# Decay factors of a gated DeltaNet: from triangle products on TensorE to running sums, a broadcast by way of DRAM, and an exponential with a bias per token

## The chip, the cores and the metric

The kernel runs on one core of a Trainium2 chip. The metric is the time of one execution in device microseconds (us), as the median of several runs. The profile shows one execution of the same program; its engines are called PE (TensorE, with PEld for its weight loads), DVE (VectorE), ACT (ScalarE), POOL (GpSimd) and SP (SyncE, which issues most of the DMAs).

## The reference

One decoder layer on 256 tokens of 2048 channels in float32: RMSNorm, one input projection, two token mixers side by side, gates, an output projection, and then a gated MLP of width 5632. What the change touches lies in the first mixer, a gated delta rule with 16 heads of 128 channels. Per head and token there is a log decay g (never positive) and a rate beta:

```
g_log = -exp(a_log) * softplus(a_raw + dt_bias)          # (256 tokens, 16 heads)
g     = cumsum(g_log within a chunk)
decay[i, j] = exp(g[i] - g[j])   for j <= i, else 0
lmat  = strictly lower part of (beta_i k_i . k_j) * decay
attn  = (q_i . k_j) * decay
```

`lmat` goes into a triangular solve, `attn` into the output. The reference walks chunks of 64 tokens with a state between them. The decay between any two tokens, however they are chunked, is the exponential of the sum of `g_log` over the tokens after j up to i.

## The kernel before, in words

The 256 tokens are two tiles of 128 (t = 0, 1). There is no state: the kernel builds the whole 256 by 256 lower triangle of each head from two tiles, `dec0` (source token j in tile 0 on the partitions, target token i in 0 to 255 along the row) and `dec1` (source and target both in tile 1). `dec0` therefore has a triangular block (targets 0 to 127) and a full block (targets 128 to 255).

The work is a sequence of large products. `gemm_a` (L138) multiplies the 256 tokens by 512 columns of a weight matrix. Each weight piece of 256 x 512 is loaded by SP into one of four `raw` buffers (L110), cast by ACT into `whi` (L112) and its rest is taken by DVE into `wlo` (L119), with three buffers for each of the two; PE then runs twelve products of 512 columns on the piece (L149 to L151). Pieces are prepared two ahead of PE.

The mixing part runs over four groups g of four heads: K, Q, V, the pooling input, its gate, a small pooling product, Z and the other gate. The delta rule of a group is a generator, `gdn` (L445). It is stepped by `side()` twice per weight piece, so that its small products, evictions and DVE work are written between the large products. The order on each engine is not exactly the written one: a planner with its own model of the times puts an instruction where it thinks its inputs are ready, the earlier written one first, and each engine then executes its own list strictly in that order, as does SP with its DMAs.

The places that matter here:

- L294 to L304: masks made by POOL and DVE at the start. `tri` is 1 where the column is at or after the partition, `low` is 1 where the column is before it, `onesr` and `lowr` are float32r copies.
- L381: `glog`, the log decays, tokens on partitions, 2 tiles by 16 heads; it comes at the end of a chain of some 25 small DVE instructions.
- L384 to L393: `glog` split in a float32r part `ghi` and the rest `glo`, and one small product with `low` (L391) for `tail`, the sum over the tokens of tile 0 after the source token.
- L455 to L484: the decays of a group, two heads at a time. DVE multiplies `tri` by the log decay of each source token (L464, L465, four instructions for each of the two parts), PE multiplies these by `lowr` or `onesr` (L472, L473, L475: the triangle products, six for two heads), ACT takes exponentials out of PSUM (L476, L477, L480), POOL zeroes the upper triangles (L482).
- L491 and L493: products of keys with keys and queries; L506 and L510: DVE multiplies these by `dec0`, `dec1` and a factor per token.
- L520 to L568: a block inverse of the triangular matrix. It sends small tiles through DRAM (`cdd`, `lb`, `tbd`, `tct`) on SP's queue. `tct` and `tcm` share buffers with two of the products of L465.
- L654 and L716: the output `on` of a group uses the buffer of `dec0`; L716 is its last reader. `psg` is a pool of four PSUM banks that all the small products share.

Of the kernel before, what the change touches and what calls it, by code (L numbers as in the profile page):

```python
# [26 lines left out]
B0 = 32  # L27
# [6 lines left out]
def kernel(  # L34
# [20 lines left out]
    nc = tc.nc  # L55
    mm = nc.tensor.matmul
# [4 lines left out]
    dpool = ctx.enter_context(tc.tile_pool(name="dram", bufs=2, space=bass.MemoryType.DRAM))  # L61
# [118 lines left out]
    ones = cpool.tile([P, P], F32, name="ones")  # L180
# [3 lines left out]
                            channel_multiplier=1)  # L184
# [7 lines left out]
    mp = mix.__enter__()  # L192
# [17 lines left out]
    for k2 in range(KD // 2):  # L210
# [6 lines left out]
        for kk in range(2):  # L217
# [3 lines left out]
                                           op0=ALU.mult, op1=ALU.subtract)  # L221
# [59 lines left out]
    for c in range(4):  # L281
        for t in range(2):
# [8 lines left out]
    nc.vector.tensor_scalar(rsq, rs1, 0.25, None, op0=ALU.mult)  # L291


    tri = mp.tile([P, P], F32, name="tri")  # L294
    nc.gpsimd.affine_select(tri, ones, pattern=[[1, P]], compare_op=ALU.is_ge, fill=0.0, base=0,
                            channel_multiplier=-1)
    low = mp.tile([P, P], F32, name="low")
    nc.gpsimd.affine_select(low, ones, pattern=[[-1, P]], compare_op=ALU.is_gt, fill=0.0, base=0,
                            channel_multiplier=1)

    onesr = mp.tile([P, P], F32R, name="onesr")
    nc.vector.tensor_copy(onesr, ones)
    lowr = mp.tile([P, P], F32R, name="lowr")
    nc.vector.tensor_copy(lowr, low)  # L304

    def same_block(b, name, tag):
        e = mp.tile([P, P // b, b], F32, tag=tag, name=name)
# [10 lines left out]
    for cq in range(4):  # L318
        pr = slice(32 * cq, 32 * cq + 32)
        nc.gpsimd.affine_select(idb[pr], ones[pr, 0:1].unsqueeze(2).to_broadcast([32, 8, B0]),  # L320
                                pattern=[[-1, 8], [1, B0]], compare_op=ALU.is_equal, fill=0.0, base=-8 * cq,
                                channel_multiplier=0)
# [57 lines left out]
    glog = mp.tile([P, 2, NH], F32, name="glog")  # L380
    nc.vector.tensor_tensor(glog, lp, ea.unsqueeze(1).to_broadcast([P, 2, NH]), op=ALU.mult)  # L381


    ghi = mp.tile([P, 2, NH], F32R, name="ghi")  # L384
    nc.vector.tensor_copy(ghi, glog)
    glo = mp.tile([P, 2, NH], F32, name="glo")
    nc.vector.tensor_tensor(glo, glog, ghi.bitcast(F32), op=ALU.subtract)


    psd = pg([P, NH])  # L390
    mm(psd, low, glog[:, 0, :], start=True, stop=True)  # L391
    tail = mp.tile([P, NH], F32, name="tail")
    nc.vector.tensor_copy(tail, psd)  # L393

    bands = mp.tile([P, 4, NB], F32, name="bands")
    for g, win in enumerate(WINDOWS):
# [3 lines left out]
        for cs in (slice(0, P + PAD), slice(P + PAD, NB)):  # L403
            b = bd[:, cs]
            n = cs.stop - cs.start
# [39 lines left out]
    def gdn(g, kq, vT, res):  # L445
# [6 lines left out]
        sj = mp.tile([P, 2, 4], F32, tag="sj", name=nm("sj"))  # L452
        dec0 = mp.tile([P, 4, S], F32, tag="dec0", name=nm("dec0"))
        dec1 = mp.tile([P, 4, P], F32, tag="dec1", name=nm("dec1"))
        for hp in range(2):  # L455

            h0 = 2 * hp
            rx = []
            for part, gp in (("h", ghi.bitcast(F32)), ("l", glo)):
                r0 = mp.tile([P, 2, P], F32R, tag="r0" + part, name=nm("r0"))  # L460
                r1 = mp.tile([P, 2, P], F32R, tag="r1" + part, name=nm("r1"))
                for i in range(2):
                    hh = 4 * g + h0 + i
                    nc.vector.tensor_scalar(r0[:, i], tri, gp[:, 0, hh : hh + 1], None, op0=ALU.mult)  # L464
                    nc.vector.tensor_scalar(r1[:, i], tri, gp[:, 1, hh : hh + 1], None, op0=ALU.mult)  # L465
                rx.append((r0, r1))
            yield
            pd0 = pg([P, 2, P])
            pdx = pg([P, 2, P])
            pd1 = pg([P, 2, P])  # L470
            for n, (r0, r1) in enumerate(rx):
                mm(pd0, lowr, r0, start=(n == 0), stop=(n == 1))  # L472
                mm(pd1, lowr, r1, start=(n == 0), stop=(n == 1))  # L473
            for n, (r0, r1) in enumerate(rx):
                mm(pdx, onesr, r1, start=(n == 0), stop=(n == 1))  # L475
            nc.scalar.activation(dec0[:, h0 : h0 + 2, 0:P], pd0, AF.Exp)  # L476
            nc.scalar.activation(dec1[:, h0 : h0 + 2, :], pd1, AF.Exp)  # L477
            for i in range(2):
                hh = 4 * g + h0 + i
                nc.scalar.activation(dec0[:, h0 + i, P:S], pdx[:, i, :], AF.Exp, bias=tail[:, hh : hh + 1])  # L480
            for d in (dec0[:, h0 : h0 + 2, 0:P], dec1[:, h0 : h0 + 2, :]):
                nc.gpsimd.affine_select(d, d, pattern=[[0, 2], [1, P]], compare_op=ALU.is_ge, fill=0.0, base=0,  # L482
                                        channel_multiplier=-1)
            yield  # L484
        for hp in range(2):
            h0 = 2 * hp
            hs = slice(h0, h0 + 2)
# [55 lines left out]
        tbd = dpool.tile([32, 4, 8 * B0], F32, tag="tbd", name=nm("tbd"))  # L543
        for cq in range(4):
            nc.sync.dma_start(tbd[:, cq], tb[32 * cq : 32 * cq + 32].rearrange("p c i -> p (c i)"))
        tct = mp.tile([P, 8, B0], F32, tag="r1l", name=nm("tct"))
        nc.sync.dma_start(tct, tbd.rearrange("(q r) a (c i) -> q (r a c) i", q=8, i=B0).rearrange("q p i -> p q i"))

        for h in range(4):
# [5 lines left out]
                nc.scalar.activation(vt[:, t, h, :], pvt[:, t, :], AF.Copy, scale=nk[:, t, h : h + 1])  # L555
        for _ in range(WAIT - 3):
            yield
        tcm = mp.tile([P, 8, B0], F32, tag="r1h", name=nm("tcm"))
        nc.vector.transpose(tcm.rearrange("p q c -> p (q c)"), tct.rearrange("p q c -> p (q c)"))
        Ta = mp.tile([P, 8, P], F32, tag="T", name=nm("T"))  # L560
        TTa = mp.tile([P, 8, P], F32, tag="TT", name=nm("TT"))
# [342 lines left out]
```

## Time and profile before

| what | value |
|---|---|
| time, median of 3 runs | 1582.16 us (1582.14 to 1584.18) |
| the profiled execution: its own time, its span | 1581.35 us, 1579.6 us |
| mean granted TensorE clock | 0.997 |
| DVE, ACT, POOL busy | 1040.2 us (66%), 745.8 us (47%), 89.4 us (6%) |
| DMA | 314.61 MB, mean 199 GB/s |

Busy time counts an engine as occupied from the start to the modelled end of each instruction. Products on PE overlap, so that the step from one start to the next is shorter than the duration of one. A row of the groups gives line, engine, operation, tiles, shapes and count, then the total busy time, the mean of one in ns, and the idle time in front of it with the one that ended it. A row of a timeline gives start, duration up to the end of the last merged instruction, and what it is. A row of the waits gives who waited for whom, the total, the number of times and the longest.

### The profile page before, as it was taken

The page shows a single profiled execution, that of the slowest core. Times are in us where ns is not written, and L with a number is a line of the kernel's source. Part 1 is how long each engine was busy: PE and PEld are TensorE (multiplying, and loading weights), DVE is VectorE, ACT ScalarE, POOL GpSimd, SP SyncE. Part 2 cuts the span into 40 slices and gives each one's busy share as a digit, 9 for nine tenths or more (in the row PEclk, how much of TensorE's full clock was granted, in tenths as well). Part 3 has the DMA queues.
Part 4 walks back from the last instruction along what each step waited for, and adds up shares of the span by engine and source line. Part 5 has one row for each costly group of instructions (what it writes and reads, how often), then busy time and mean ns, then how long its engine had stood idle before and what let it go on. Part 6 is the DMA issues. An engine that isn't in the chain of part 4 may idle for free.

```text
span 1579.6 us, 20017 instructions
## 1 busy us (share of the span) xinstructions
PE 1556.7 (99%) x7408; PEld 1284.3 (81%) x7408; DVE 1040.2 (66%) x1544; ACT 745.8 (47%) x925; POOL 89.4 (6%) x121
## 2 busy tenths in 40 slices
PE   8999999999999999999999999999999999999997
PEld 6878888888888888787888888888788878888885
DVE  5778757786678757795655666665666666444445
ACT  6545436444545435454454455444454445434344
POOL 3020100100010100102000000000000000000000
PEclk9999999999999999999999999999999999999998
DMA  7656656665556655565555878788777787755553
GB/s 253 181 155 195 193 148 173 167 197 173 155 153 190 197 149 175 164 191 176 198 188 187 238 224 243 242 244 247 232 234 251 230 246 234 239 196 191 196 191 132
DMA packets 263736, 314.61 MB, mean 199 GB/s; under 512 B 109894, under 2 KB 124246, under 8 KB 263510
## 3 DMA queue, kind: packets, MB, share of 16 engines
q1 hardware_dynamic: 260928, 308.85, 64.5%
q10 hardware_dynamic: 2710, 4.48, 0.8%
q8 instruction: 58, 0.95, 0.2%
q14 instruction: 40, 0.33, 0.1%
HBM read 298.61 MB, written 14.68 MB: 198 GB/s over the span
## 4 chain that ended last, share of the span: by engine, by line
PE 86%; DMA 4%; DVE 4%; issue 3%; SPq 1%; POOL 1%; ACT 0%; DVEq 0%; POOLq 0%
PE psm L151 22%; PE psm L150 21%; PE psm L149 21%; PE psg L840 3%; PE psm L839 3%; PE psg L839 2%; PE psm L838 2%; PE psg L838 2%; PE psm L840 2%; DVE wlo L119 2%; DMA gs<-flip 1%; SPq L162 1%; PE psg L491 1%; DMA flip<-tn 1%; PE psg L175 1%
## 5 line engine op out<-in xcount | busy, mean ns | idle before, releaser
L119 DVE TENSOR_TENSOR wlo<-raw,whi 128x1024 fp32r<-128x1024 f32 x528 | 648.5, 1233 | 376.1 <-ACT whi L112 368.6
L112 ACT CAST whi<-raw 128x1024 fp32r<-128x1024 f32 x530 | 556.9, 1053 | 716.2 <-PE psm L150 548.2
L151 PE MATMUL psm<-wlo,xhl 128*128 128x512 f32 x896 | 353.1, 394 | 2.1 <-DVE wlo L119 2.1
L149 PE MATMUL psm<-whi,xhl 128*128 128x512 f32 x896 | 352.3, 393 | 1.3 <-ACT xhl L219 1.3
L150 PE MATMUL psm<-whi,xhl 128*128 128x512 f32 x896 | 351.9, 393 | 0.0
L151 PE MATMUL psm<-wlo,fhl 128*128 128x512 f32 x704 | 273.7, 390 | 1.9 <-DVE wlo L119 1.4
L150 PE MATMUL psm<-whi,fhl 128*128 128x512 f32 x704 | 274.0, 389 | 0.0
L149 PE MATMUL psm<-whi,fhl 128*128 128x512 f32 x704 | 273.9, 389 | 0.0
L151 PEld LDWEIGHTS psm<-wlo,xhl 128*128 128x128 f32 x896 | 168.6, 188 | 37.8 <-DVE wlo L119 3.7
L149 PEld LDWEIGHTS psm<-whi,xhl 128*128 128x128 f32 x896 | 168.7, 188 | 35.4 <-ACT xhl L219 1.7
L150 PEld LDWEIGHTS psm<-whi,xhl 128*128 128x128 f32 x896 | 168.7, 188 | 34.7
L151 PEld LDWEIGHTS psm<-wlo,fhl 128*128 128x128 f32 x704 | 132.1, 188 | 32.0 <-DVE wlo L119 4.8
L150 PEld LDWEIGHTS psm<-whi,fhl 128*128 128x128 f32 x704 | 132.2, 188 | 27.6
L149 PEld LDWEIGHTS psm<-whi,fhl 128*128 128x128 f32 x704 | 132.2, 188 | 27.1
L838 PE MATMUL psg<-whi,hhi 128*128 128x512 f32 x176 | 68.5, 389 | 0.0
L838 PE MATMUL psm<-whi,hhi 128*128 128x512 f32 x176 | 68.5, 389 | 0.0
L839 PE MATMUL psm<-whi,hlo 128*128 128x512 f32 x176 | 68.5, 389 | 0.0
L839 PE MATMUL psg<-whi,hlo 128*128 128x512 f32 x176 | 68.5, 389 | 0.0
L840 PE MATMUL psm<-wlo,hhi 128*128 128x512 f32 x176 | 68.5, 389 | 0.0
L840 PE MATMUL psg<-wlo,hhi 128*128 128x512 f32 x176 | 61.1, 389 | 0.0
L439 DVE SCALAR_TENSOR_TENSOR cy<-psg,cqw,cy 128x255 f32<-128x255 f32 (+1 forms) x144 | 60.5, 473 | 0.4 <-ACT cy L436 0.4
L151 PE MATMUL psm<-wlo,mhi 128*128 128x512 f32 x128 | 50.0, 391 | 0.3 <-DVE wlo L119 0.3
(223 smaller groups left out, 1351.7 us busy)
## 6 DMA issues: line engine op xcount, KB each, us to landing
raw<-in_w_in_dram SPq DMA_DIRECT2D x226, 512.0 KB, 3.9
raw<-in_w_up_dram SPq DMA_DIRECT2D x176, 512.0 KB, 4.5
raw<-in_w_down_dram SPq DMA_DIRECT2D x88, 512.0 KB, 4.5
raw<-in_w_out_dram SPq DMA_DIRECT2D x32, 512.0 KB, 3.5
flip<-tn SPq DMA_DIRECT2D x88, 128.0 KB, 4.7
gs<-flip SPq DMA_DIRECT2D x22, 512.0 KB, 4.7
raw<-in_pool_w_dram SPq DMA_DIRECT2D x8, 512.0 KB, 4.1
x<-in_x_dram SPq DMA_DIRECT2D x4, 512.0 KB, 6.9
```

The lines of the kernel that those rows point to most:

```text
L112: nc.scalar.copy(hi, raw)
L119: nc.vector.tensor_tensor(lo, raw, hi.bitcast(F32), op=ALU.subtract)
L149: mm(ps[:, t, :], lh(k, t), hi[:, kk, :], start=(k == 0), stop=False)
L150: mm(ps[:, t, :], ll(k, t), hi[:, kk, :], start=False, stop=False)
L151: mm(ps[:, t, :], lh(k, t), lo[:, kk, :], start=False, stop=(k == nk - 1))
L162: nc.sync.dma_start(dv[a], b[32 * a : 32 * a + 32].rearrange("p t (f j) -> p t f j", j=32))
L175: nc.tensor.transpose(pt[:, ff, t * P : (t + 1) * P], src[:, t, f * P : (f + 1) * P], ident)
L439: nc.vector.scalar_tensor_tensor(y[:, f, s:], gs[:, : S - s], w(j), y[:, f, s:], op0=ALU.mult, op1=ALU.add)
L491: mm(pg0, kq[:, h, 0, 0:P], kq[:, h, :, :], start=True, stop=True)
L838: mm(acc[c][t], lh(k, t), hi[:, kk, :], start=(k == 0), stop=False)
L839: mm(acc[c][t], ll(k, t), hi[:, kk, :], start=False, stop=False)
L840: mm(acc[c][t], lh(k, t), lo[:, kk, :], start=False, stop=(k == KF - 1))
```

## The change

The decays are no longer formed by products of triangles. With `run[i]` the running sum of `glog` over the tokens of i's own 64 (the first token of each 64 starts anew), the decay of a pair is exp(run[i] + shift[j]), and the shift depends on the source token j and on which of the four 64s the target lies in. Before the groups begin, two float32 products make the running sums with heads on partitions (`psr`), DVE copies them to SBUF (`runs`), and SP writes them to DRAM (`rund`, 16 KB). Five small float32 products make six columns of shifts for all 16 heads (`shift`). Per group, SP then reads four rows of `rund` onto all 128 partitions, straight into `dec0` (512 KB written); POOL puts -1e30 over the upper triangles of `dec0` and, taking the second half of it, of `dec1`; ACT takes the exponential in place in 24 instructions of 128 x 64, each with its column of `shift` as the bias.

The masks at the start change: POOL makes `low`, then `tri` with one quadrant zeroed, `ntri`, `ntail` and `top`; DVE no longer makes `onesr` and `lowr`. The generator has as many steps as before (four before the key products). `tct` and `tcm` get buffers of their own. The core of the diff:

```diff
+    nc.gpsimd.memset(tri[0:64, 64:P], 0.0)
+    ntri = mp.tile([P, P], F32, name="ntri")
+    nc.gpsimd.tensor_scalar(ntri, tri, -1.0, None, op0=ALU.mult)
+    ntail = mp.tile([P, P], F32, name="ntail")
+    nc.gpsimd.tensor_copy(ntail, ntri)
+    nc.gpsimd.tensor_copy(ntail[0:64, 0:64], low[0:64, 0:64])
+    top = mp.tile([P, P], F32, name="top")
+    nc.gpsimd.memset(top, 0.0)
+    nc.gpsimd.memset(top[0:64], 1.0)
-    onesr = mp.tile([P, P], F32R, name="onesr")
-    nc.vector.tensor_copy(onesr, ones)
-    lowr = mp.tile([P, P], F32R, name="lowr")
-    nc.vector.tensor_copy(lowr, low)
...
-    nc.vector.tensor_copy(ghi, glog)
-    nc.vector.tensor_tensor(glo, glog, ghi.bitcast(F32), op=ALU.subtract)
-    psd = pg([P, NH])
-    mm(psd, low, glog[:, 0, :], start=True, stop=True)
-    nc.vector.tensor_copy(tail, psd)
+    psr = pg([NH, S])
+    for t in range(2):
+        mm(psr[:, t * P : (t + 1) * P], glog[:, t, :], tri, start=True, stop=True)
+    runs = mp.tile([NH, S], F32, name="runs")
+    nc.vector.tensor_copy(runs, psr)
+    rund = dpool.tile([NH, S], F32, tag="rund", bufs=1, name="rund")
+    nc.sync.dma_start(rund, runs)
+    pse = pg([P, 6, NH])
+    for n, mat in ((0, ntri), (2, ntail)):
+        mm(pse[:, n : n + 2, :], mat, glog, start=True, stop=True)
+    mm(pse[:, 4, :], low, glog[:, 0, :], start=True, stop=True)
+    mm(pse[:, 5, :], low, glog[:, 0, :], start=True, stop=False)
+    mm(pse[:, 5, :], top, glog[:, 1, :], start=False, stop=True)
+    shift = mp.tile([P, 6, NH], F32, name="shift")
+    nc.vector.tensor_copy(shift, pse)
...
-        for hp in range(2):
-            h0 = 2 * hp
-            rx = []
-            for part, gp in (("h", ghi.bitcast(F32)), ("l", glo)):
-                r0 = mp.tile([P, 2, P], F32R, tag="r0" + part, name=nm("r0"))
-                r1 = mp.tile([P, 2, P], F32R, tag="r1" + part, name=nm("r1"))
-                for i in range(2):
-                    hh = 4 * g + h0 + i
-                    nc.vector.tensor_scalar(r0[:, i], tri, gp[:, 0, hh : hh + 1], None, op0=ALU.mult)
-                    nc.vector.tensor_scalar(r1[:, i], tri, gp[:, 1, hh : hh + 1], None, op0=ALU.mult)
-                rx.append((r0, r1))
-            yield
-            pd0 = pg([P, 2, P])
-            pdx = pg([P, 2, P])
-            pd1 = pg([P, 2, P])
-            for n, (r0, r1) in enumerate(rx):
-                mm(pd0, lowr, r0, start=(n == 0), stop=(n == 1))
-                mm(pd1, lowr, r1, start=(n == 0), stop=(n == 1))
-            for n, (r0, r1) in enumerate(rx):
-                mm(pdx, onesr, r1, start=(n == 0), stop=(n == 1))
-            nc.scalar.activation(dec0[:, h0 : h0 + 2, 0:P], pd0, AF.Exp)
-            nc.scalar.activation(dec1[:, h0 : h0 + 2, :], pd1, AF.Exp)
-            for i in range(2):
-                hh = 4 * g + h0 + i
-                nc.scalar.activation(dec0[:, h0 + i, P:S], pdx[:, i, :], AF.Exp, bias=tail[:, hh : hh + 1])
-            for d in (dec0[:, h0 : h0 + 2, 0:P], dec1[:, h0 : h0 + 2, :]):
-                nc.gpsimd.affine_select(d, d, pattern=[[0, 2], [1, P]], compare_op=ALU.is_ge, fill=0.0, base=0,
-                                        channel_multiplier=-1)
-            yield
+        nc.sync.dma_start(dec0, rund[4 * g : 4 * g + 4, :].partition_broadcast(P))
+        yield
+        for d, src in ((dec1, dec0[:, :, P:S]), (dec0[:, :, 0:P], dec0[:, :, 0:P])):
+            nc.gpsimd.affine_select(d, src, pattern=[[0, 4], [1, P]], compare_op=ALU.is_ge, fill=-1e30, base=0,
+                                    channel_multiplier=-1)
+        yield
+        for h in range(4):
+            hh = 4 * g + h
+            for d, n in ((dec0[:, h, 0:64], 0), (dec0[:, h, 64:P], 2), (dec0[:, h, P : P + 64], 4),
+                         (dec0[:, h, P + 64 : S], 5), (dec1[:, h, 0:64], 1), (dec1[:, h, 64:P], 3)):
+                nc.scalar.activation(d, d, AF.Exp, bias=shift[:, n, hh : hh + 1])
+            if h % 2:
+                yield
...
-        tct = mp.tile([P, 8, B0], F32, tag="r1l", name=nm("tct"))
+        tct = mp.tile([P, 8, B0], F32, tag="tct", name=nm("tct"))
...
-        tcm = mp.tile([P, 8, B0], F32, tag="r1h", name=nm("tcm"))
+        tcm = mp.tile([P, 8, B0], F32, tag="tcm", name=nm("tcm"))
```

More of the change, by code (lines that the diff above doesn't have):

```diff
@@ L291 @@
     nc.vector.tensor_scalar(rsq, rs1, 0.25, None, op0=ALU.mult)
+    low = mp.tile([P, P], F32, name="low")
+    nc.gpsimd.affine_select(low, ones, pattern=[[-1, P]], compare_op=ALU.is_gt, fill=0.0, base=0,
+                            channel_multiplier=1)
     tri = mp.tile([P, P], F32, name="tri")
@@ L296 @@
                             channel_multiplier=-1)
-    low = mp.tile([P, P], F32, name="low")
-    nc.gpsimd.affine_select(low, ones, pattern=[[-1, P]], compare_op=ALU.is_gt, fill=0.0, base=0,
-                            channel_multiplier=1)
-    onesr = mp.tile([P, P], F32R, name="onesr")
-    nc.vector.tensor_copy(onesr, ones)
-    lowr = mp.tile([P, P], F32R, name="lowr")
-    nc.vector.tensor_copy(lowr, low)
+    nc.gpsimd.memset(tri[0:64, 64:P], 0.0)
[7 more added lines that the diff above has]
+    nc.gpsimd.memset(top[0:64], 1.0)
     def same_block(b, name, tag):
@@ L381 @@
     nc.vector.tensor_tensor(glog, lp, ea.unsqueeze(1).to_broadcast([P, 2, NH]), op=ALU.mult)
-    ghi = mp.tile([P, 2, NH], F32R, name="ghi")
-    nc.vector.tensor_copy(ghi, glog)
-    glo = mp.tile([P, 2, NH], F32, name="glo")
-    nc.vector.tensor_tensor(glo, glog, ghi.bitcast(F32), op=ALU.subtract)
-    psd = pg([P, NH])
-    mm(psd, low, glog[:, 0, :], start=True, stop=True)
-    tail = mp.tile([P, NH], F32, name="tail")
-    nc.vector.tensor_copy(tail, psd)
+    psr = pg([NH, S])
[13 more added lines that the diff above has]
+    nc.vector.tensor_copy(shift, pse)
     bands = mp.tile([P, 4, NB], F32, name="bands")
```

## The prediction, made before the changed kernel ran

> **What bounds the kernel now.** I read the page first, for which engine has no idle time; then PE's waits, for what little it loses; then PE's timeline around the products that go, for what one of them really takes.
>
> ```profile
> span 1579.6 us, 20017 instructions
> PE 1556.7 (99%) x7408; PEld 1284.3 (81%) x7408; DVE 1040.2 (66%) x1544; ACT 745.8 (47%) x925; POOL 89.4 (6%) x121
> q1 hardware_dynamic: 260928, 308.85, 64.5%
> ```
>
> ```profile
> PE psg L206 <- DMA nmrows<-in_norm_mix_w_dram: 4.6, 1, 4.6
> PE psm L151 <- DVE wlo L119: 3.7, 8, 0.9
> PE psg L215 <- DMA x<-in_x_dram: 1.5, 2, 0.9
> PE psm L149 <- ACT xhl L219: 1.3, 1, 1.3
> PE psg L580 <- POOL T L565: 0.7, 1, 0.7
> ```
>
> PE is busy 99% of the span, and the second block is the whole list of its waits: 11.8 us, of which 7.4 (the first, third and fourth rows) belong to the start. So almost any time that leaves PE's list leaves the run, and any wait that is put into it is added. The trap is the size of a product: busy time counts each from start to modelled end, and these overlap.
>
> ```profile
> 79.45 0.39 PE L149 MATMUL psm<-whi,xhl 128*128 128x512 f32 x1
> 79.68 0.40 PE L472 MATMUL psg<-r,lowr 128*128 128x256 f32 x2
> 79.92 0.39 PE L150 MATMUL psm<-whi,xhl 128*128 128x512 f32 x1
> 67.25 0.29 PE L391 MATMUL psg<-glog,low 128*128 128x16 f32 x2
> 67.39 1.07 PE L175 MATMUL psg<-ident,ev 128*128 128x128 f32 x8
> ```
>
> Two triangle products start at 79.68 and the next large product at 79.92: 0.24 us for two, 0.12 each in PE's stream, though each is recorded at 0.28 and more. A large product takes 0.23 (79.45 to 79.68), not its recorded 0.39. These steps are the price of PE work below.
>
> **What PE loses.**
>
> ```profile
> L472 PE MATMUL psg<-r,lowr 128*128 128x256 f32 x16 | 4.6, 297 | 0.0
> L473 PE MATMUL psg<-r,lowr 128*128 128x256 f32 x16 | 4.3, 297 | 0.0
> L475 PE MATMUL psg<-r,onesr 128*128 128x256 f32 x16 | 3.5, 281 | 0.0
> ```
>
> 48 triangle products at 0.12 are 5.8 us, and L391 (67.25 to 67.39) is 0.14: together 5.9 us. No idle time stands before these groups, so no wait of PE goes with them.
>
> **What PE gains.** Two float32 products of 128 columns (`psr`) and five of 32 or 16 columns (`pse`), once. A float32 product appears as two records.
>
> ```profile
> 135.98 0.39 PE L684 MATMUL psg<-bands,ev 128*128 128x128 f32 x2
> 136.21 0.41 PE L686 MATMUL psg<-bands,ev 128*128 128x144 f32 x2
> 47.29 1.07 PE L348 MATMUL psg<-id,bat 64*128 64x32 f32 x8
> 48.30 0.50 PE L150 MATMUL psm<-whi,xhl 128*128 128x512 f32 x1
> ```
>
> A float32 product of 128 columns takes 0.23 us (135.98 to 136.21), so `psr` is 0.5. For the ten records of `pse` the near rows are L391 (0.07 a record) and L348 (1.01 us for eight, 0.126 a record): 0.7 to 1.3, I take 1.0, between them, since they have 16 and 32 columns like those two. Added: 1.5 us. They take the place of L391 in the order, where no wait of PE is listed, so I expect none. PE's balance is 5.9 - 1.5 = **4.4 us less**.
>
> **DVE's relief.**
>
> ```profile
> L465 DVE TENSOR_SCALAR r<-tri,glo 128x128 fp32r<-128x128 f32 x16 | 10.1, 666 | 3.6 <-POOL TT L565 3.6
> L464 DVE TENSOR_SCALAR r<-tri,glo 128x128 fp32r<-128x128 f32 x16 | 4.3, 307 | 0.0
> L464 DVE TENSOR_SCALAR r<-tri,ghi 128x128 fp32r<-128x128 f32 x16 | 4.1, 291 | 3.7 <-PE psg L472 3.7
> L465 DVE TENSOR_SCALAR r<-tri,ghi 128x128 fp32r<-128x128 f32 x16 | 3.9, 275 | 0.0
> ```
>
> DVE loses 22.4 us of work and 7.3 us of waiting; the 3.6 came from the buffers that `tct` shared. DVE is no bound, and what this can give PE is at most its 3.7 us of waits for `wlo`, which are spread over the whole span. I take 0.4, about a tenth. The copies of `runs` and `shift` are two small instructions in place of four.
>
> **ACT.** Per group, 24 exponentials of 128 x 64 replace eight.
>
> ```profile
> L480 ACT ACTIVATE dec<-psg,tail 128x128 f32<-128x128 f32 x16 | 5.0, 363 | 0.0
> L476 ACT ACTIVATE dec<-psg 128x256 f32<-128x256 f32 x8 | 3.1, 384 | 1.2 <-PE psg L472 1.2
> 231.24 1.05 ACT L112 CAST whi<-raw 128x1024 fp32r<-128x1024 f32 x1 [1.67 <-PE psm L150]
> 233.96 1.06 ACT L112 CAST whi<-raw 128x1024 fp32r<-128x1024 f32 x1 [1.67 <-PE psm L150]
> 240.00:275.00 35.00, 35.00 (x172) 29.25 (x171) 28.80 (x52) 21.93 (x35) 2.59 (x4) 1.00 0.61 171
> ```
>
> The nearest row with a bias per token is L480, 0.36 us at twice the width, and that is the upper end: 24 x 0.36 = 8.6 us a group, where L476, its twin L477 (taken as equal) and L480 took 3.0. The cover is the idle time in which ACT waits for PE to free a buffer, 1.67 us in each period of 2.72 (last cast rows). In the 35 us where group 1 makes its decays ACT is busy 21.93 (the window row: after the length come PE, PEld, DVE, ACT, POOL, clock, DMA share), so 13 us are idle against at most 5.6 more. Each instruction is short, so a cast is put off by at most 0.36. I count nothing. Were the cover gone, 5.6 us a group would appear in the casts.
>
> **The path through DRAM.** It adds five DMAs to SP's queue. The nearest rows are the loads of 512 KB through DRAM in the MLP, and for the waits behind such transfers DVE's:
>
> ```profile
> gs<-flip SPq DMA_DIRECT2D x22, 512.0 KB, 4.7
> cdd<-cd SPq DMA_DIRECT2D x4, 128.0 KB, 4.3
> L482 POOL TENSOR_SCALAR_AFFINE_SELECT dec<-dec 128x256 f32<-128x256 f32 x16 | 12.0, 757 | 196.7 <-ACT dec L476 178.6 <-ACT dec L477 18.1
> 233.47 1.22 DVE L716 TENSOR_TENSOR sz<-on,sz 128x1024 f32<-128x1024 f32 x1
> 278.04 0.75 DVE L506 SCALAR_TENSOR_TENSOR ga<-psg,sj,dec 128x512 f32<-128x512 f32 x1
> ```
>
> From issue to `dec1` and `dec0` ready: 4.7 us for the transfer, two selects of twice L482's size (1.5 each, so 3.0), 8.6 of exponentials: 16.3 us. In group 1 the buffer of `dec0` is free at 234.7 (L716 ends) and first needed at 278.04 (L506), 43 us later. Group 0 has 4.3 us more for the write of `rund` and starts when L391 did, at 67. Slack is not the question. What may cost is the order: SP, POOL and ACT each execute a planned list. SP stands still for `runs` and then for the landing of `rund`, with weight loads queued behind; POOL stands for `dec0`, with nothing urgent behind; ACT stands for POOL, with the casts of the weights behind, and PE waits for those. The same kind of stall is in this trace, on DVE, where the planner thought a transfer would land sooner:
>
> ```profile
> DVE y L797 <- DMA gs<-flip: 23.1, 11, 3.7
> 127.36 0.42 DVE L538 TENSOR_TENSOR tmp<-lb,tb 128x248 f32<-128x248 f32 x1 [3.40 <-DMA lb<-cdd]
> 128.90 0.39 PE L150 MATMUL psm<-whi,xhl 128*128 128x512 f32 x1
> 129.75 0.50 PE L151 MATMUL psm<-wlo,xhl 128*128 128x512 f32 x1 [0.46 <-DVE wlo L119]
> ```
>
> DVE's stall of 3.40 us up to 127.36 shows in PE as a step of 0.85 instead of 0.23: 0.62 lost. So the two pieces prepared ahead absorb about 2.8 us, and the rest passes to PE. A stall of ACT of 2 to 3.7 us in each of four groups would cost between nothing and 0.9 each. I take 0.1 a group, 0.4, near the lower end because the average of DVE's eleven waits on the first row is 2.1, under 2.8; 3.6 goes into the range. SP's own stall I count at nothing: four `raw` buffers lie between it and ACT.
>
> **The start.** POOL has six more small instructions, ahead of the band masks in the written order.
>
> ```profile
> 8.42 2.72 POOL L408 TENSOR_SCALAR_AFFINE_SELECT bands<-bands 128x144 f32<-128x144 f32 x6
> 10.60 0.88 DVE L410 TENSOR_TENSOR bands<-bands,ident 128x128 f32<-128x128 f32 x3
> ```
>
> The six selects of L408 end at 11.14 (0.45 a step), the DVE instructions that take them stand among the first `xlo` rows. Six steps of a quarter to a half us put the masks off by up to 3 us; DVE's order would be replanned with it. Between 0 and 3 us; I take 0.2, since the masks are not needed before the first pooling product at 136 us and DVE loses two casts here.
>
> **The sum.** -4.4 - 0.4 + 0.4 + 0.2 = -4.2 us. The profiled execution has 1581.35 us (1.75 beyond its span) and would come to 1577.2. The median stands 0.81 above it, so 1582.16 - 4.2 = **1578.0 us**. What a measurement of this kernel can tell from no change is about 0.2%, 3.2 us: faster is below 1579.0, slower above 1585.3.
>
> **The rivals.**
>
> *Waits give most of it back.* ACT's stalls at 0.9 a group (3.6) and the start at 1 us give 1582.16 - 4.8 + 4.6 = 1582.0. For it speak DVE's stalls of 3.40 and 3.7 above; against it that ACT's instructions here can be planned anywhere in 43 us.
>
> *ACT stands for the whole chain (slower).* If the exponentials are in ACT's list right behind the issue of the transfer, ACT waits for the transfer and both selects, 7.7 us, with the casts behind; PE loses 7.7 - 2.8 = 4.9 in each of four groups, 19.6, and the time is 1582.16 - 4.8 + 19.6 = 1597.0. It decides the sign from a stall of 4.0 us on (2.8 + 4.8 / 4). For it speaks that the generator steps from transfer to selects to exponentials with one step each, against it that the longest stall of this kind here is 3.7.
>
> *The transfers are not hidden.* Four times 512 KB are 2.1 MB more on the queue that brings the weights. At the 171 GB/s of the window row, were DMA the bound, that is 12.3 us, 1589.7. Against it stand the DMA share of 0.61 there and a list of PE's waits with no weight load in it. The Trainium skill, page "DMA: Bandwidth & Descriptors", section "Issuing engines are not separate DMA queues", says that transfers started by any engine interleave on the same sixteen DMA engines; by that rule no choice of queue would get these 2.1 MB out of the way of the weights. The share of 0.61 agrees that it can matter only if the idle 0.39 is used up.
>
> *A product counts in full.* If each of the 48 is worth its recorded 0.28 to 0.30 us, PE loses 14.0 us and the time is 1582.16 - 14.0 + 1.5 = 1569.7. The steps in PE's timeline speak against it. The Trainium skill, page "Perfetto Trace Analysis", section "Identifying the Most-Contended Engine", warns that matmul busy time misjudges TensorE because matmuls are pipelined; the steps of 0.12 against a mean of 297 ns agree with it.
>
> **How the numbers follow.** My forecast, 1575.0 to 1579.0, has 0.56; waits that give it back 0.24; ACT's long stall 0.11; exposed transfers 0.04; products in full 0.05. Faster is then 0.61, same 0.24, slower 0.15. The range of 8 in 10 is 1574.0 to 1586.0: it leaves out the products in full and most of the two slower cases, and takes in the waits at their upper bound.
>
> **What would show it.** Right: PE's instructions fall from 7408 by 50 - 14 = 36 and its waits stay near 12 us; the steps around the new float32 products are 0.07 to 0.12 a record; the casts (L112) wait for PE as before; ACT's exponentials take 0.25 to 0.36 each; the selects take 1 to 1.5; `dec0` lands 4 to 6 us after its issue. Wrong: a row in PE's waits on `wlo` or `whi` of more than 4 us inside the four groups, an ACT wait on POOL's select of over 4 us, or an L410 that holds the start.

## The result: 1595.1 us, slower by 0.7%, and the profile after

The changed kernel takes 1595.1 us (median; 1591.97 to 1595.67), the kernel before 1583.2 beside it: a ratio of 1.0071 [1.0057, 1.0085], about 12 us slower. The forecast was 4.2 us faster, and the time lies 9 us above the top of the range. The profiled execution took 1595.01 us, 13.7 more than the profiled one of before. The page after has this in its head and in its engine and queue rows:

```profile
span 1592.4 us, 19939 instructions
PE 1559.0 (98%) x7372; PEld 1280.1 (80%) x7372; DVE 1028.0 (65%) x1477; ACT 759.1 (48%) x989; POOL 92.9 (6%) x119
q1 hardware_dynamic: 261536, 310.96, 64.3%
```

The work fell as meant: PE has 36 instructions fewer, DVE 12 us less, ACT 13 us more. Much of the time is in PE's waits (who for whom: total, times, longest). Their list was 11.8 us long before and is 22.6 now; the rows of the start have not changed (7.4 and 7.5). These three have:

```profile
PE psm L151 <- DVE wlo L119: 5.5, 12, 1.5
PE psg L569 <- POOL T L554: 4.6, 5, 1.5
PE psm L149 <- ACT whi L112: 4.2, 5, 2.3
```

One row is new and one has grown most: PE waits for ACT's casts (`whi`, 4.2 us, of which 3.3 at the decays and 0.9 in the output projection), and for POOL's products `T` (4.6; 0.7 before). ACT's timeline and PE's of group 0 show where the first comes from:

```profile
72.99 1.04 ACT L112 CAST whi<-raw 128x1024 fp32r<-128x1024 f32 x1
...
76.02 4.42 ACT L471 ACTIVATE dec<-dec,shift 128x64 f32<-128x64 f32 x18 [1.62 <-POOL dec L464]
...
81.06 0.58 ACT L471 ACTIVATE dec<-dec,shift 128x64 f32<-128x64 f32 x2
...
82.48 1.05 ACT L471 ACTIVATE dec<-dec,shift 128x64 f32<-128x64 f32 x4
83.44 2.93 ACT L112 CAST whi<-raw 128x1024 fp32r<-128x1024 f32 x3
```

```profile
81.82 0.39 PE L151 MATMUL psm<-wlo,xhl 128*128 128x512 f32 x1
84.52 0.50 PE L149 MATMUL psm<-whi,xhl 128*128 128x512 f32 x1 [2.32 <-ACT whi L112]
```

ACT waits 1.62 us for the select, then runs 18, 2 and 4 exponentials and some work of the convolution, in the order of its list. Between the cast at 72.99 and the next at 83.44 lie 9.4 us without a cast, and PE stands at 82.2 until the end of that one. The two pieces prepared ahead were used up.

The second shows in DVE's and POOL's timelines where group 1 multiplies out `T`; first the kernel before, then after:

```profile
356.58 2.55 POOL L565 TENSOR_TENSOR T<-tcm,eb 128x512 f32<-128x512 f32 x2
356.65 2.56 DVE L465 TENSOR_SCALAR r<-tri,glo 128x128 fp32r<-128x128 f32 x2 [1.19 <-POOL TT L565]
359.13 1.21 DVE L119 TENSOR_TENSOR wlo<-raw,whi 128x1024 fp32r<-128x1024 f32 x1
```

```profile
358.83 4.36 DVE L119 TENSOR_TENSOR wlo<-raw,whi 128x1024 fp32r<-128x1024 f32 x2
362.08 4.50 POOL L554 TENSOR_TENSOR T<-tcm,eb 128x512 f32<-128x512 f32 x2
363.12 1.21 DVE L697 SCALAR_TENSOR_TENSOR sz<-gate,psm 128x1024 f32<-128x1024 f32 x1
```

Two `T` products take 4.50 us in place of 2.55, and the two casts of DVE (`wlo`), which run beside POOL's products, some 2.2 each, where the cast at 359.13, with POOL idle, takes 1.21. Before, DVE stood for POOL (1.19) because the `r` tiles shared their buffers with `tct`, and then worked on two triangles; after, that wait is gone and DVE works right through POOL's products. The kernel before had the same thing in its last group, where no next group's triangles follow; POOL's and PE's timelines there:

```profile
720.01 4.48 POOL L565 TENSOR_TENSOR T<-tcm,eb 128x512 f32<-128x512 f32 x2
```

```profile
724.55 0.44 PE L580 MATMUL psg<-T,ga 32*32 32x32 f32 x16 [0.73 <-POOL T L565]
```

By stage, from the starts of the first product of the output projection, of the MLP, and of its last part (PE's timeline of before, then of after):

```profile
747.95 0.48 PE L149 MATMUL psm<-whi,mhi 128*128 128x512 f32 x1
...
845.88 0.39 PE L149 MATMUL psm<-whi,fhl 128*128 128x512 f32 x1
...
1326.85 0.39 PE L838 MATMUL psg<-whi,hhi 128*128 128x512 f32 x1
```

```profile
756.06 0.39 PE L149 MATMUL psm<-whi,mhi 128*128 128x512 f32 x1
...
855.85 0.39 PE L149 MATMUL psm<-whi,fhl 128*128 128x512 f32 x1
...
1339.00 0.39 PE L827 MATMUL psg<-whi,hhi 128*128 128x512 f32 x1
```

The groups end 8.1 us later, the output projection adds 1.9 and the MLP, whose code is the same, 2.2. Of the 1.9, 0.9 is only moved: eight records of group 3's product of `vt` and `TT` stand behind this boundary here and ahead of it in the kernel before. PE has 4.2 us less to do in the groups, so some 13 us were lost there (8.1 + 0.9 + 4.2).

### The profile page after: what moved, and what is told of

Read it like the earlier page. It is cut to its first block, busy times and chain, and to the rows that moved or that the text cites. A ratio compares the mean times of both kernels' runs of the same rounds, so it can differ in the third digit from the quotient of the medians.

```text
span 1592.4 us, 19939 instructions
## 1 busy us (share of the span) xinstructions
PE 1559.0 (98%) x7372; PEld 1280.1 (80%) x7372; DVE 1028.0 (65%) x1477; ACT 759.1 (48%) x989; POOL 92.9 (6%) x119
## 3 DMA queue, kind: packets, MB, share of 16 engines
q10 hardware_dynamic: 2710, 4.48, 0.8%
## 4 chain that ended last, share of the span: by engine, by line
PE 77%; DMA 5%; DVE 4%; ACT 3%; POOL 2%; issue 2%; SPq 1%; POOLq 0%; DVEq 0%; ACTq 0%
PE psm L151 20%; PE psm L149 19%; PE psm L150 19%; PE psm L829 2%; PE psg L828 2%; PE psg L827 2%; PE psm L827 2%; PE psm L828 2%; PE psg L829 2%; DVE wlo L119 2%; ACT whi L112 1%; DMA gs<-flip 1%; POOL T L554 1%; ACT dec L471 1%; DMA dec<-rund 1%
## 5 line engine op out<-in xcount | busy, mean ns | idle before, releaser
L445 DVE SCALAR_TENSOR_TENSOR cy<-psg,cqw,cy 128x255 f32<-128x255 f32 (+2 forms) x144 | 60.7, 474 | 4.8 <-ACT cy L442 4.7
L149 PE MATMUL psm<-whi,mhi 128*128 128x512 f32 x128 | 50.3, 393 | 0.9 <-ACT whi L112 0.9
```

Source lines behind the costliest of these rows:

```text
L149: mm(ps[:, t, :], lh(k, t), hi[:, kk, :], start=(k == 0), stop=False)
L445: nc.vector.scalar_tensor_tensor(y[:, f, s:], gs[:, : S - s], w(j), y[:, f, s:], op0=ALU.mult, op1=ALU.add)
```

## The experiments

My theory after this reading: two side effects, which add. **(A)** ACT's wait for the select and its long run of exponentials come together out of the lead that the two prepared pieces give (the lead is the time from the end of a cast to the first product on it). **(B)** The buffers of `tct` and `tcm`, now their own, free DVE to run beside POOL's `T`, which slows both. Rivals: the number of exponentials alone, the wait alone, the transfers through DRAM, or simply another order of the lists. All results in one table; the ratio is to the kernel before in the same set of runs, the waits (total, times) are PE's, from one profile each:

| kernel | ratio [95%] | waits for `whi` | of these at the decays | waits for `T` |
|---|---|---|---|---|
| after | 1.0071 [1.0057, 1.0085] | 4.2 (5) | 3.3 (4) | 4.6 (5) |
| after, a second time | 1.0087 [1.0072, 1.0102] | 4.6 (4) | 3.7 (3) | 5.0 (5) |
| before, own buffers | 1.0022 [1.0006, 1.0038] | none | none | 5.1 (4) |
| before, 24 exponentials | 0.9989 [0.9977, 1.0001] | 0.9 (1) | none | 1.5 (1) |
| after, triangles kept on DVE | 1.0048 [1.0031, 1.0065] | 4.4 (5) | 3.5 (4) | 0.7 (1) |
| after, shift added by DVE | 1.0017 [1.0004, 1.003] | 0.9 (1) | none | 5.3 (4) |
| after, rows read early | 1.0032 [1.0017, 1.0048] | 1.6 (2) | 0.7 (1) | 5.5 (4) |
| after, `T` on DVE | 1.0047 [1.0032, 1.0063] | 3.5 (3) | 3.5 (3) | none |
| after, shift and `T` on DVE | 0.9963 [0.995, 0.9975] | none | none | none |
| before, own buffers, `T` on DVE | 0.9977 [0.9966, 0.9987] | none | none | none |
| both on DVE, 24 exponentials | 0.9971 [0.9952, 0.999] | none | none | none |
| rows early, `T` on DVE | 0.9982 [0.9971, 0.9993] | 0.4 (1) | 0.4 (1) | none |
| both on DVE, 24 with a bias | 0.9988 [0.9974, 1.0003] | none | none | none |

Where a wait for `whi` is not at the decays, it is one of 0.91 us in the output projection.

**The second side effect alone, on the kernel before.**

```
-  tct = mp.tile([P, 8, B0], F32, tag="r1l", ...)     +  ... tag="tct"
-  tcm = mp.tile([P, 8, B0], F32, tag="r1h", ...)     +  ... tag="tcm"
```

> The kernel before, with one part of the change: tct and tcm get buffers of their own, so that DVE's first triangle instructions of the next group no longer stand still until POOL has read tct. Theory B (the sharing kept DVE out of POOL's way while POOL makes T; in the changed kernel both run at once, and each is slowed): POOL's products into T go from 1.5 us each to about 2.2, DVE's casts beside them from 1.2 to about 2.0, PE waits 3 to 5 us in all for T instead of 0.7, and the time is 3 to 6 us above the kernel before. Rival C (nothing but the planner's order moves, and it moves by chance): no wait on T, within 2 us of before. If sharing only cost time, as my prediction had it: up to 1 us faster.

Slower by 0.22%, 3.5 us. POOL's group of this kernel, and that of the kernel before:

```profile
L565 POOL TENSOR_TENSOR T<-tcm,eb 128x512 f32<-128x512 f32 x8 | 18.0, 2266 | 0.0
```

```profile
L565 POOL TENSOR_TENSOR T<-tcm,eb 128x512 f32<-128x512 f32 x8 | 12.1, 1532 | 0.0
```

Two tags, no other edit, and `T` takes 2266 ns in place of 1532. Taking away a wait of DVE made the kernel slower.

**The number of exponentials alone, on the kernel before.** Its exponentials out of PSUM are cut into 24 per group, each with a bias column (`tail`, or zeros).

```
for i in range(2):
    for c in (slice(0, 64), slice(64, P)):
        for d, ps, b in ((dec0[:, h0+i, 0:P], pd0, zero), (dec1[:, h0+i, :], pd1, zero),
                         (dec0[:, h0+i, P:S], pdx, tail[:, hh:hh+1])):
            nc.scalar.activation(d[:, c], ps[:, i, c], AF.Exp, bias=b)
```

> The kernel before, with its eight exponentials of a group cut into 24 of 128 x 64, each with a bias per token, from PSUM as before: the ACT work of the change without its path through DRAM. Theory A (ACT's many short instructions stand in a block in front of the casts of the weights, and PE runs dry): PE waits on whi or wlo near the decays of each group, 1 us or more a group, 4 to 6 us above the kernel before. Theory A2 (what costs is ACT standing for the select and the transfer ahead of the block, not the number of instructions): within 2 us of before. Theory B says nothing of this run.

No slower. ACT's timeline of group 0 has blocks of four with casts between them (in groups 1 to 3 they are blocks of eight, 2 us):

```profile
80.41 0.93 ACT L483 ACTIVATE dec<-psg,zero 128x64 f32<-128x64 f32 x4 [1.18 <-PE psg L474]
81.21 1.07 ACT L112 CAST whi<-raw 128x1024 fp32r<-128x1024 f32 x1
```

PE has no wait for `whi` at the decays. So the price of ACT's extra work is nothing where it comes in pieces of 1 to 2 us.

**The second side effect taken out of the kernel after.** DVE still multiplies out the 64 triangles of L464 and L465, which nobody reads, and `tct` and `tcm` share their buffers with them again.

> The changed kernel, with DVE's triangle instructions of before kept although nothing reads them (16 per group and part, 22 us of DVE work in all), and tct and tcm sharing their buffers again. Theory B: more DVE work makes it faster, by 3 to 5 us, because POOL's T products fall back to about 1.3 to 1.5 us and PE's waits on T from 4.6 to under 1.5 us. Rival C, or T being late for another reason: not faster, 0 to 4 us slower than the changed kernel. Theory A's waits (about 6 us around the decays) stay.

POOL's group and PE's wait row:

```profile
L567 POOL TENSOR_TENSOR T<-tcm,eb 128x512 f32<-128x512 f32 x8 | 12.1, 1538 | 0.0
```

```profile
PE psg L582 <- POOL T L567: 0.7, 1, 0.7
```

`T` is back at 1538 ns and PE's wait at 0.7, while the waits for `whi` stay (4.4). DVE has more work, and the kernel is 0.2 to 0.4% faster than after by the two measurements of that one, with intervals that overlap for the first of them.

**The first side effect taken out of the kernel after.** DVE adds the shift, and ACT takes two exponentials per group without a bias.

```
nc.vector.tensor_tensor(d3, d3, s3.unsqueeze(2).to_broadcast([P, 4 * nb, 64]), op=ALU.add)
nc.scalar.activation(d, d, AF.Exp)          # once for dec0, once for dec1
```

> The changed kernel, with the shift added by DVE (one instruction of 128 x 1024 and one of 128 x 512 per group) and two exponentials on ACT without bias per token instead of 24. ACT's work per group falls from about 6 us to 1.7. Theory A: the waits of PE around the decays (about 6 us in all, 3.2 in group 0) fall to 1 to 2, and the time is 4 to 5 us below the changed kernel, 1587 to 1592 on the scale where before has 1583. Theory A2 (the wait for transfer and select is what costs): at most 2 us below the changed kernel, since that wait stays. PE's waits on T stay at about 4.6 us by either.

No wait for `whi` is left at the decays, and the time falls to 1.0017; the waits for `T` stay (5.3). The transfers and the selects are still there. ACT's wait is not what it was, though: it waits for DVE's addition, 3.7 us in all, where the kernel after waits 8.9 for the select.

```profile
ACT dec L474 <- DVE dec L473: 3.7, 5, 1.0
```

So this run takes away the long block and most of the wait at once and does not price them apart. The time falls by 0.54 to 0.70%, 8.5 to 11 us, against the two measurements of after. That is more than the 4 to 5 expected, and more than the 5.8 us by which PE's steps around the decays are too long in the profile of after. In the second profile of after a lowered clock adds up to 3.4 us there (shown at the end); beyond that no run shows where the rest comes from.

**The transfer brought forward.** The rows are read into a buffer of their own, so that SP can issue the read before `dec0` is free; selects and exponentials read from there.

```
rb = mp.tile([P, 4, S], F32, tag="rb", bufs=1);  nc.sync.dma_start(rb, rund[...].partition_broadcast(P))
```

> The changed kernel, with the rows of a group read into a buffer of their own instead of into dec0. From group 1 on the transfer is done long before dec0 is free, so that ACT's wait for the transfer goes; the 24 exponentials stay and are still ready all at once. Group 0 has no such lead. Theory A2 (ACT's wait for transfer and select does the harm): PE's waits around the decays of groups 1 to 3, 2.6 us in the changed kernel, fall under 0.5, those of group 0 (3.2 us) stay, and the time is about 2 us below the changed kernel. Theory A (a block of many exponentials that are ready at once is put in front of the casts, with or without the wait): the waits of groups 1 to 3 stay above 1.5 us and the time is within 1 us of the changed kernel. The waits on T (4.6 us) stay by both.

More than half of the loss goes (1.0032): 6 to 9 us, where about 2 were expected. In groups 1 to 3 ACT no longer waits for the transfer, only 1.46 us for the select, and its block stands elsewhere (from 230.6 us on in group 1, where after has it from 243.4). There a piece is ready at least 3.2 to 3.7 us before PE takes it, in place of 0.05 to 0.37 after; since the wait and the place of the block changed together, the run does not say which of them did it. In group 0 nothing can be earlier, and the lead is 0.05 as in the kernel after. The times of this version scatter from 1583.74 to 1595.71 us, and the profile is of the fastest execution, so its waits explain the median only in part.

**`T` on DVE, in the kernel after.** `nc.gpsimd.tensor_tensor` becomes `nc.vector.tensor_tensor` at L554.

> The changed kernel, with the four products per group that make T and TT moved from POOL to DVE. Theory B (POOL and DVE slow each other while both run there): PE's waits on T go from 4.6 us to under 1, DVE's casts beside them are back at 1.2 us, and the time is 3 to 6 us below the changed kernel, although DVE has some 10 us more work. If the late T came from its place in the order and not from both engines running at once: PE's waits on T stay above 3 us.

```profile
L554 DVE TENSOR_TENSOR T<-tcm,eb 128x512 f32<-128x512 f32 x8 | 5.1, 686 | 0.0
```

DVE's group: 686 ns against POOL's 2145, and no wait for `T` is left. The ratio falls only to 1.0047, since (A) is still there (`whi` 3.5, and `wlo` 7.1).

**Both at once:** the shift added by DVE and `T` on DVE.

> The two remedies together: the shift added on DVE with two exponentials on ACT, and T and TT made on DVE. If theories A and B are the whole of what the path of the change costs, the waits around the decays and on T are both under 1.5 us in all, and what remains against before is the 4.4 us of PE work saved less 1 to 2 us of other waits: 2 to 4 us faster than the kernel before, a ratio of 0.9975 to 0.9990. If the rest of the loss is spread by the planner's chance (rival C): within 0.2% of before.

0.9963: faster than the kernel before, and by 1.1 to 1.2% than the kernel after. This is PE's whole list of waits:

```profile
PE psg L206 <- DMA nmrows<-in_norm_mix_w_dram: 3.5, 1, 3.5
PE psg L215 <- DMA x<-in_x_dram: 2.5, 2, 1.8
PE psm L151 <- DVE wlo L119: 2.4, 5, 1.0
PE psm L149 <- ACT xhl L219: 1.7, 1, 1.7
```

Three of the four rows are of the start. Alone the two edits gave 0.54 to 0.70% and 0.24 to 0.40% (against the two measurements of after), together 1.08 to 1.24: they add, or a little more.

**How much of that belongs to the old kernel.** Before, with own buffers and `T` on DVE.

> The kernel before, with tct and tcm in buffers of their own as in the first run, and T and TT made on DVE. Theory B: the 5.1 us of waits on T that the first run showed go under 1, and the time is back at the kernel before, within 2 us, below it rather than above. If the wait on T came from the order alone: as the first run, 2 to 5 us above before.

0.9977: 3.6 us come from `T` alone, more than the 2 expected, and that is why the version with both gained 5.9 us where 2 to 4 were expected. The change itself, with the shift added by DVE and without its side effects, is worth 0.9963 against 0.9977, some 2.2 us, and the intervals overlap; the 4.4 us less of PE work is neither shown nor excluded by that.

**Count without wait, wait without count.** In the version with both, the exponentials are cut into 24 again, without a bias, behind DVE's addition.

> The version with both remedies, with its two exponentials per group cut into 24 of 128 x 64 again (no bias per token: the shift is still added on DVE). The theory by now: neither ACT's wait nor the number of instructions costs anything alone; PE runs dry where wait and block together put two casts of ACT more than about 5.4 us apart (two pieces of 2.72 us). Here wait and block stand together again: the distance of casts over the decays of groups 0 to 3 is back above 5.5 us, PE's waits there are 3 to 7 us in all, and the time is 3 to 7 us above the version with two exponentials. If only the wait on the transfer counted, or the bias per token: within 1.5 us of that version.

I had expected 3 to 7 us lost, as in the kernel after. Nothing was (0.9971), though all 24 of group 0 stand in one block. ACT's timelines, of this kernel and of a further one in which each exponential has a column of zeros as its bias:

```profile
76.89 3.62 ACT L477 ACTIVATE dec<-dec 128x64 f32<-128x64 f32 x24
```

```profile
77.43 5.86 ACT L479 ACTIVATE dec<-dec,zero 128x64 f32<-128x64 f32 x24 [0.26 <-DVE dec L475]
```

> The version with both remedies and 24 exponentials per group, with a bias per token added to each (a column of zeros, so that only the form of the instruction changes). Without it one took 0.15 us in a row, in the changed kernel 0.245 with it: 24 x 0.095 = 2.3 us more of ACT per group. The theory by now is a budget: a piece of the weights is normally cast 4.4 us before PE uses it, ACT's wait and its block of exponentials come out of that together, and PE loses only what goes beyond. In the run before this one the least lead in groups 0 to 3 was 2.7, 1.5, 1.7 and 1.3 us, and PE lost nothing. With 2.3 us more it goes to about 0.4, 0, 0 and 0: PE waits on whi or wlo at the decays come back, 2 to 5 us in all, and the time is 2 to 5 us above the version without bias (1577.6 beside a before of 1583.2). If the wait for the transfer were the whole cause: no wait at the decays, within 1.5 us of that version.

A bias column costs 0.09 us an instruction (5.86 / 24 = 0.244 against 0.151). The Trainium skill, page "ScalarE: Activation LUTs", section "What ACT_TABLE_LOAD costs", prices a pointer operand at about 93 ns and the overlap in a row at the same; an estimate from that page's figures gives 0.24 us with and 0.15 without for 64 elements, and these runs agree. The lead of group 0 is at least 4.4 us in the kernel before; the block of 3.62 leaves 2.73 of it, that of 5.86 with its wait of 0.26 leaves 0.22. The second is longer by 2.24 and waits 0.26 more, and the lead is shorter by 2.51, as it would be if block and wait add. PE's waits for `wlo` go from 3.1 to 8.2 us, of which 2.4 stand behind the four blocks (none there without the bias):

```profile
PE psm L151 <- DVE wlo L119: 8.2, 14, 1.3
```

The time rises by 0.17%, 2.7 us, but the two intervals overlap. For the lead it is the length of the block that counts, with the wait ahead of it, and not the number of instructions.

**Transfer early and `T` on DVE.**

> The changed kernel with its 24 biased exponentials, the rows read early into a buffer of their own, and T and TT made on DVE. By the theory the block without most of the wait stays under 5.4 us between casts in groups 1 to 3, and T is not late: PE's waits at the decays are those of group 0 alone, about 1.8 us, and on T under 0.5; the time is 1 to 3 us above the version with two exponentials, that is 2 to 5 us below the kernel before. If the number of instructions counted by itself, as in theory A: 5 us or more above the version with two exponentials.

0.9982, faster than before although the 24 exponentials keep their bias. In groups 1 to 3 they stand in blocks of 8 and 16 without a wait ahead, and the lead there is 3.1 us or more; in group 0 it is 0.05.

**The kernel after once more.**

> The changed kernel once more, as it is, beside the two above on the same chip: a ratio of 1.005 to 1.009 to the kernel before by its first measurement, waits of PE at the decays of 5 to 7 us in all and on T of 4 to 6 us.

It agrees with the first measurement, and its profile shows the same two waits (4.6 and 5.0).

## Why the prediction was wrong, step by step

**Right in the main.** PE's instructions fell by 36, though its waits did not stay near 12 us, as was named for a sign (22.6). The new float32 products took 1.7 us in PE's timeline (1.5 forecast), `psr` 0.54 and `pse` 1.13:

```profile
67.64 0.61 PE L390 MATMUL psg<-tri,glog 128*16 128x128 f32 x4
68.18 0.41 PE L397 MATMUL psg<-glog,ntri 128*128 128x32 f32 x2
...
69.31 0.42 PE L175 MATMUL psg<-ident,ev 128*128 128x128 f32 x2
```

The transfer landed 4.3 us after its issue in group 0 and 4.1 to 4.9 in the others (4.7 forecast), an exponential steps at 0.245 (18 in 4.42; up to 0.36 forecast), and the two selects take 1.2 us together, where 3.0 were forecast. POOL's groups and ACT's waits:

```profile
L464 POOL TENSOR_SCALAR_AFFINE_SELECT dec<-dec 128x512 f32<-128x512 f32 x8 | 4.9, 635 | 81.9 <-DMA dec<-rund 81.9
```

```profile
ACT dec L471 <- POOL dec L464: 8.9, 4, 2.7
```

ACT waits 2.2 us a group on average (1.62 to 2.72), about the 2 to 3.7 that were named. The transfers are hidden: queue q1 has the same share and PE has no wait for weights. The masks at the start show no cost.

**The step that failed first: "Each instruction is short, so a cast is put off by at most 0.36. I count nothing."** It assumes that the planner puts a cast between any two exponentials. It put 18 in a row in group 0 and 11 and 7 in group 1, behind a wait:

```profile
243.39 2.74 ACT L471 ACTIVATE dec<-dec,shift 128x64 f32<-128x64 f32 x11 [2.68 <-POOL dec L464]
246.03 1.04 ACT L112 CAST whi<-raw 128x1024 fp32r<-128x1024 f32 x1
246.97 1.78 ACT L471 ACTIVATE dec<-dec,shift 128x64 f32<-128x64 f32 x7
...
251.75 1.99 ACT L112 CAST whi<-raw 128x1024 fp32r<-128x1024 f32 x2
```

```profile
252.85 0.50 PE L149 MATMUL psm<-whi,xhl 128*128 128x512 f32 x1 [0.35 <-ACT whi L112]
```

**The lead.** Worked out piece by piece, it is at least 4.4 us around the decays of the kernel before (elsewhere in the groups it falls to 2.4); after, it falls to 0.05, 0.05, 0.37 and 0.05 in the four groups, and PE's steps around the decays are 5.8 us too long in all (3.2 in group 0). The prediction priced wait and exponentials apart, each against the whole of the cover: the wait at 0.4, the exponentials at nothing. They come out of the same 4.4 us. What the experiments show of it: 24 in pieces of 1 to 2 us cost nothing, 24 with a bias in one block and almost no wait leave 0.2, and waits of up to 1.7 us with two exponentials (the version with both) leave 3.1 or more. A wait as long as after's, up to 2.7 us, without the block was not run.

**The second: DVE's relief.** "The 3.6 came from the buffers that `tct` shared" was read rightly and booked as a pure loss of DVE. It was also what kept DVE's two-input casts off POOL's `T`. The row was there to be read: the mean of 1532 ns hides 2.53 to 2.55 us for two in groups 0 to 2 and 4.48 in group 3, the only group with no triangles behind it. After, the four groups have 3.48 to 4.52, and PE loses about 5 us in and behind these waits (1.7 of them at the lowered clock shown below) where the prediction had a gain of 0.4. The own buffers alone, on the kernel before, show 3.5 us of it.

**The account of the groups,** from PE's steps in single profiles: 4.2 us of work less, 5.8 more at the decays, 5.2 at `T` (after it 7.4, before 2.2), and about 1.4 in stalls behind the small transfers `lb`; together 8.2. The rows above have 8.1, or 9.0 with the eight moved records, so some 0.8 is not accounted for.

**The rivals.** That ACT stands for the whole chain gave 1597.0, near the time, but for a stall of 7.7 us a group that isn't there; the near hit isn't its merit. "Waits give most of it back" had the right kind of cause at 0.9 a group, against some 1.5 that were lost to ACT, and 5.2 in all to POOL, which it didn't have at all. The transfers in full are refuted by the last versions, which keep them and are faster than before. The products in full are refuted by the 2.2 us between the version with both and the kernel before with own buffers and `T` on DVE, where that rival has 12.5.

**What stays open.** The output projection took 97.9 us from its first product to that of the MLP in eight of the profiles and 99.8 in six, among them both of after, the 24 exponentials on the kernel before, and three more variants. The traces show what it is: in the six, the eight records of group 3 stand behind its first product (0.9 us), and PE waits 0.91 us for a cast of ACT, a wait that none of the eight has. Which order the planner chooses, and why, no run isolates; it also happens without the path through DRAM. The MLP's part took 478.5 to 484.1 us over the profiles with the same code, so the 2.2 there can't be laid to the change. Every edit also gives the planner another order of all lists, and no run holds that order fixed; what speaks against chance is that the waits for `T` and the leads move each time as the edit would have them.

## What to carry to other kernels

Where work is prepared ahead, measure the lead in us (end of the preparing instruction to first use), and charge to it the wait and the whole block of instructions that an in-order list can put ahead of the next preparation, together. Before a wait of a side engine is counted as loss, look at what runs on the other engine at that moment: an instance without the wait, like the last round of a loop, shows what it costs to be without it. A group's mean over eight instances is not a price until the instances agree.

## What the hardware showed

`T` on POOL, two inputs of 128 x 512, takes 1.27 us beside DVE's triangles and 2.25 where DVE runs two-input instructions throughout; the DVE casts go from 1.22 to 2.2. Beside POOL a triangle on DVE takes 1.28 in place of 0.3, so there DVE pays and POOL does not. The single instructions look as if the one that begins second stood until the first is done: in group 1 of after a cast ends at 363.20, and the `T` begun at 362.08 ends 1.15 later; the next cast ends at 365.46, and the `T` begun at 364.31 ends 1.12 later. DVE's `sz` at 363.12, which reads one input from PSUM, is not slowed (1.21). The Trainium skill, page "GPSIMD Engine Reference", section "Specifications", says that GPSIMD shares its SBUF interfaces with VectorE and contends with DVE instructions in a 2-port perf mode or with two SBUF inputs; the casts, which read `raw` and `whi`, agree. The triangles have one tensor input, and in which mode they ran no run here shows. On DVE the product `T` takes 0.69 us.

After the wait of 1.52 us for `T` in group 1 PE also ran slowly for a while. PE's timeline and the window from 364 to 371 us (length, PE, PEld, DVE, ACT, POOL, granted clock, DMA share, GB/s):

```profile
366.63 0.44 PE L569 MATMUL psg<-T,ga 32*32 32x32 f32 x16 [1.52 <-POOL T L554]
367.00 0.79 PE L151 MATMUL psm<-wlo,xhl 128*128 128x512 f32 x1
367.60 0.63 PE L149 MATMUL psm<-whi,xhl 128*128 128x512 f32 x1
368.02 0.63 PE L150 MATMUL psm<-whi,xhl 128*128 128x512 f32 x1
...
370.53 0.40 PE L150 MATMUL psm<-whi,xhl 128*128 128x512 f32 x1
```

```profile
364.00:371.00 7.00, 5.48 (x47) 4.13 (x46) 3.66 (x3) 2.12 (x6) 2.58 (x2) 0.76 0.78 223
```

Eight products take 3.53 us (367.00 to 370.53) in place of 1.84, six of them at steps of 0.42 to 0.43 in place of 0.23, which costs another 1.7 us. The granted clock is 0.50 for 3.4 us there (0.76 over the 7 us of the window). A wait of 1.50 us at 552 in the same profile had no such sequel.

This is a part of the price that no wait lists. In the second profile of after it stands behind PE's stall in group 0 as well, here for 6.8 us:

```profile
84.90:91.50 6.60, 5.59 (x12) 3.97 (x13) 5.90 (x8) 3.67 (x6) 0.00 (x0) 0.50 0.47 141
```

Away from the end of the span, the granted clock is 0.50 for 3.4 us in the profile of after, 10.2 in its second one, 6.8 with the triangles kept, and 3.4 each with the shift added by DVE, with `T` on DVE, and with 24 exponentials on the kernel before. In the other eight profiles, the kernel before and the version with both among them, it is never lowered there. The length of the stall does not decide it: PE's 2.32 us in group 0 of after had no such sequel, the 1.28 us for `T` in group 1 with the shift added by DVE had one.
